# Recording the mixing's instructions and ordering them with a list scheduler; the output projection in two rounds

## The chip, the cores and the metric

The kernel runs on one core of one Trainium2 chip. The metric is the device time of one execution in microseconds (us). The engines are TensorE (PE, with its weight loads PEld), VectorE (DVE), ScalarE (ACT), GpSimd (POOL) and SyncE (SP), which here only starts transfers. Each engine works through a queue of its own in a fixed order, and waits at the head of it until the work that the instruction needs is done.

## The reference

One step of a trunk of two layers, for 128 context tokens and 256 latent tokens of width 1024 (T = 384 tokens in all). A layer is a gated feed-forward half step (FFN), a token mixing, and a second FFN half step. Abridged to what matters here, the mixing is:

```python
a_q, a_k, a_v, b_q, b_k, b_v, b_g, b_r, c_q, c_k, c_v = jnp.split(h @ lp['w_in'], offs, axis=-1)
a_q = rms_norm(a_q.reshape(B, T, A_HEADS, A_HEAD_DIM), lp['g_a_q'])     # also a_k, c_q, c_k
...
out_a = gqa_attention(a_q, keys_a, vals_a)                              # 6 heads of 64
o_b, s_f, s_b = gla_bidir(b_q, b_k, b_v, log_a[:, :, 0], log_a[:, :, 1], s0[:, 0], s0[:, 1])
out_b = rms_norm(o_b, lp['g_gla']) * jax.nn.silu(b_r)                   # 4 heads, keys 32, values 64
out_c = rms_norm(diff_attention(c_q, keys_c, vals_c, lam), lp['g_c_out']) * (1.0 - lam_init)
out = jnp.concatenate([out_a, out_b, out_c], axis=-1) @ lp['w_out']
```

Everything is float32. The output is y for both groups of tokens, the new caches and the states of the gated linear attention (GLA).

## The kernel before

The program is ffn, mixing, ffn for each layer, one after the other. The large products are done with split numbers: `load_split` (line 297) loads a weight tile `wraw`, ACT rounds it to a high part `whi` (line 303) and DVE subtracts to get the low part `wlo` (line 304); `mm3` (line 307) then adds three matmuls, high by high, high by low and low by high. Such a product has `whi` or `wlo` among its names and uses the whole array of 128 by 128.

The mixing (line 561) consists of named stages. "br bq bk bv" and "wa wv wq wk" are input projections; "ha hb" make the normalised tokens `h`; "lg de st" make the decays and states of the GLA, "L0" to "L6" its scores by seven levels of halving (`gla_level`, line 912) and "go" its output; "ra rq rk" are norm and rotary embedding; "p0a" to "p2b" and "o0" to "o2" are the attention of mixer A, "ax cx c0" to "c3", "n0 n1 s0 s1" that of mixer C. The stages are called in the order of the list `ORDER` (line 63, one list for each layer), and the output projection (from line 1070) follows: for each of eight tiles of 128 outputs, nine pieces of the mixed tokens are multiplied in one accumulation, in the order of `KORD`, with two weight loads (320 KB and 256 KB).

The attention and GLA use plain float32 matmuls, many of them on a part of the array only. A profile names the part before the shape. `32*64` stands for 32 rows and 64 columns: the GLA scores (line 902, six for each head and level) and part of its output (lines 960, 963). `64*128` are the attention scores (lines 732, 742, 776, 790). `128*64` are the products with the values of A and of the GLA (lines 757, 759, 957), and `128*32` are a few GLA products (lines 849, 882). Transposes (lines 721, 1003, 1036) and the products of mixer C with its values (lines 802, 804) use all rows and more than 64 columns, as the split products do. A plain float32 matmul leaves two records in the trace, a transpose or a split product one. The PSUM tiles that the matmuls write to are called `mm`, `ax`, `both` and `ada`; they are eight banks in all.

Other lines that the change touches: `newton` (line 312) computes 1/sqrt of small tiles on DVE with 13 instructions; `rsq_bcast` (line 331) and `qk_norm` (line 656) call it. `gla_level` takes four differences of prefix sums on DVE (lines 924 to 927). `a_probs` scales the probabilities on DVE (line 747, chosen by `NRM`). `add_x` (line 421) adds a finished output tile to the residual with two DVE instructions (line 423). `make_rstd` (line 374) is called ahead of the stages.

The instructions of the stages were given to the Tile framework in the order of the program, and each engine's queue came from that.

Of the kernel before, what the change touches and what calls it, by code (L numbers as in the profile page):

```python
# [17 lines left out]
P = 128  # L18
# [17 lines left out]
# column layout of the constant pack (shape constants)  # L36
# [6 lines left out]
# column layout of the small input pack  # L43
# [12 lines left out]
# modulation vectors computed beside each FFN: vectors, units left for the down part, steps of either part  # L56
# [4 lines left out]
NRM = (0, 1)  # L61
HV = (1, 1, 1, 1, 1, 1, 1, 1)
ORDER = (
    ("ha br bq hb bk wq bv lg rq de wk st L0 rk L1 cx wa wv L2 c0 L3 c1 L4 c2 ra L5 L6 n0 s0 c3 n1 p0a ax "
     "s1 p0b p1a go o0 p1b p2a o1 p2b o2").split(),
    ("br ha hb bq bk bv lg L0 wq rq wk de L1 st rk L2 wa cx wv L3 c0 ra L4 c1 c2 L5 c3 n0 L6 p0a p0b ax "
     "p1a o0 go s0 p1b p2a p2b o1 n1 s1 o2").split(),
)
KORD = (
    ("c0 c1 c2 c3 b0 b1 a0 a1 a2").split(),  # L70
    ("a0 b0 b1 c0 c1 a1 c2 c3 a2").split(),
)
# [9 lines left out]
def _build(ctx, tc, nc, I, O):  # L82
    V, S, G, PE = nc.vector, nc.scalar, nc.gpsimd, nc.tensor

    const = ctx.enter_context(tc.tile_pool(name="const", bufs=1))
    xp = ctx.enter_context(tc.tile_pool(name="xp", bufs=1))
    hp = ctx.enter_context(tc.tile_pool(name="hp", bufs=NHP))
    wp = ctx.enter_context(tc.tile_pool(name="wp", bufs=1))
    np_ = ctx.enter_context(tc.tile_pool(name="nrm", bufs=1))
    ps_mm = ctx.enter_context(tc.tile_pool(name="psm", bufs=3, space=PSUM))  # L90
    ps_ax = ctx.enter_context(tc.tile_pool(name="psx", bufs=3, space=PSUM))
    ps_ad = ctx.enter_context(tc.tile_pool(name="psa", bufs=1, space=PSUM))

    # eight banks: three for products, three for the rest, one for either (turn), one for the modulation
# [19 lines left out]
    nc.sync.dma_start(out=cc, in_=I["sp"][:, S_C:S_C + 16])  # L114
# [12 lines left out]
    def load_consts(i):  # L127
        for t, n, c in ((sp, "sp", S_GV), (cst, "cst", K_BON)):
            cols = slice(c, None) if i else slice(0, c)
            nc.sync.dma_start(out=t[:, cols], in_=I[n][:, cols])  # L130

    def load_consts2(w):
# [6 lines left out]
        # -(exp(lq1 . lk1) - exp(lq2 . lk2) + init)  # L139
# [12 lines left out]
    # ---------------------------------------------------------------- adaLN  # L152
# [39 lines left out]
    def cond_rows_pe(pool):  # L192
# [6 lines left out]
        for r in (0, 32):  # L199
            nc.sync.dma_start(out=cb[r:r + 1], in_=I["cb"][0:1])  # L200
# [1020 lines left out]
```

## Time and profile before

| | before |
|---|---|
| time, median of 3 runs (lowest, highest) | 1599.53 us (1589.74, 1602.13) |
| span of the profiled execution | 1590.9 us |
| PE busy over the span | 1556.5 us (98%) |
| DVE, ACT, POOL busy | 1236.2, 726.6, 196.5 us |
| the two mixings, from 317 to 536 us and from 1096 to 1311 us | 219 and 215 us |
| an FFN between them, 536 to 818 us | 282 us |

The page gives no time for the profiled execution other than its span. A matmul's record lasts until its result has been written, so the records of successive matmuls overlap; how long one of them keeps PE is the time from its start to the start of the next. PE "busy" therefore says little by itself: a stretch in which no new matmul starts for 0.3 us still counts as busy.

### The profile page before, as it was taken

How to read it: one execution, taken by the hardware profiler on the slowest of the kernel's cores; microseconds unless marked ns; L12 is line 12 of the kernel's file. 1: busy time of each engine (PE TensorE's matmuls, PEld its weight loads, DVE VectorE, ACT ScalarE, POOL GpSimd, SP SyncE). 2: the span in 40 equal slices, each digit the busy share in tenths (PEclk: the TensorE clock that was granted, in tenths of full speed). 3: DMA queues.
4: the chain of work that ended last, by engine and by line, in shares of the span. 5: the costliest groups of instructions: out<-in, count | busy, mean ns of one | idle time of the engine just before them, and what ended most of it. 6: DMA issues, size and time to landing. Idle time of an engine off the chain costs nothing.

```text
span 1590.9 us, 25045 instructions
## 1 busy us (share of the span) xinstructions
PE 1556.5 (98%) x9370; PEld 1457.3 (92%) x9370; DVE 1236.2 (78%) x2318; ACT 726.6 (46%) x1420; POOL 196.5 (12%) x239
## 2 busy tenths in 40 slices
PE   7999999999999999999999999999999999999999
PEld 4999999987667999999999999999875599999999
DVE  4799999888876788988968988676897867666532
ACT  4544433356566544443344444334646554444321
POOL 1111130031000211111001111101100011111100
PEclk9999999999899999999999999999999999999999
DMA  8666677533103465566655556543321064433441
GB/s 327 222 228 227 226 225 253 182 98 114 48 7 130 163 204 198 198 196 198 216 212 202 196 198 203 178 136 117 116 77 39 1 232 148 143 133 132 124 139 56
DMA packets 83229, 256.37 MB, mean 161 GB/s; under 512 B 10978, under 2 KB 19746, under 8 KB 82722
## 3 DMA queue, kind: packets, MB, share of 16 engines
q1 hardware_dynamic: 83108, 254.78, 48.2%
q8 instruction: 73, 1.20, 0.3%
q14 instruction: 48, 0.39, 0.1%
HBM read 251.99 MB, written 2.75 MB: 160 GB/s over the span
## 4 chain that ended last, share of the span: by engine, by line
PE 88%; DVE 7%; ACT 2%; issue 1%; DMA 1%; POOL 1%; SPq 0%; DVEq 0%; ACTq 0%; POOLq 0%
PE mm L308 20%; PE mm L309 20%; PE mm L310 20%; PE both L308 6%; PE both L310 6%; PE both L309 6%; DVE wlo L304 1%; PE mm L742 1%; PE mm L790 1%; DVE t L686 1%; PE ax L721 1%; DVE junk L254 1%; PE ax L804 1%; PE ax L902 0%; ACT p L697 0%
## 5 line engine op out<-in xcount | busy, mean ns | idle before, releaser
L303 ACT ACTIVATE whi<-wraw 128x1024 fp32r<-128x1024 f32 (+4 forms) x358 | 348.3, 974 | 457.3 <-PE mm L309 265.5
L304 DVE TENSOR_TENSOR wlo<-wraw,whi 128x1024 fp32r<-128x1024 f32 (+4 forms) x358 | 452.4, 1266 | 132.6 <-ACT whi L303 131.4
L310 PE MATMUL mm<-h,wlo 128*128 128x386 f32 x1112 | 379.2, 341 | 2.3 <-DVE wlo L304 2.3
L308 PE MATMUL mm<-h,whi 128*128 128x386 f32 x1112 | 378.4, 341 | 2.8 <-POOL h L367 1.4
L309 PE MATMUL mm<-h,whi 128*128 128x386 f32 x1112 | 377.9, 340 | 0.5 <-POOL h L367 0.3
L254 DVE SCALAR_TENSOR_TENSOR junk<-araw,cb 128x1024 f32<-128x1024 f32 x256 | 312.6, 1221 | 0.8
L308 PEld LDWEIGHTS mm<-h,whi 128*128 128x128 f32 x1112 | 210.8, 190 | 5.0 <-ACT whi L303 1.9
L310 PEld LDWEIGHTS mm<-h,wlo 128*128 128x128 f32 x1112 | 211.0, 190 | 3.9 <-DVE wlo L304 3.3
L309 PEld LDWEIGHTS mm<-h,whi 128*128 128x128 f32 x1112 | 211.1, 190 | 2.1 <-POOL h L367 0.8
L477 POOL TENSOR_TENSOR alo<-s,ahi 128x384 fp32r<-128x384 f32 x88 | 115.6, 1314 | 641.7 <-ACT ahi L475 615.1
L309 PE MATMUL mm<-alo,whi 128*128 128x384 f32 x528 | 177.9, 337 | 0.0
L310 PE MATMUL mm<-ahi,wlo 128*128 128x384 f32 x528 | 177.9, 337 | 0.0
L308 PE MATMUL mm<-ahi,whi 128*128 128x384 f32 x528 | 177.9, 337 | 0.0
L308 PE MATMUL both<-h,whi 128*128 128x386 f32 x344 | 117.0, 340 | 0.0
L310 PE MATMUL both<-h,wlo 128*128 128x386 f32 x344 | 116.7, 339 | 0.0
L309 PE MATMUL both<-h,whi 128*128 128x386 f32 x344 | 116.5, 339 | 0.0
L475 ACT ACTIVATE ahi<-s 128x384 fp32r<-128x384 f32 x88 | 46.3, 526 | 129.4 <-DVE s L472 129.3
L308 PEld LDWEIGHTS mm<-ahi,whi 128*128 128x128 f32 x528 | 99.2, 188 | 0.0
L309 PEld LDWEIGHTS mm<-alo,whi 128*128 128x128 f32 x528 | 99.2, 188 | 0.0
L310 PEld LDWEIGHTS mm<-ahi,wlo 128*128 128x128 f32 x528 | 99.2, 188 | 0.0
L308 PE MATMUL mm<-whi,h 128*128 128x384 f32 (+2 forms) x240 | 86.6, 364 | 6.2 <-ACT bc L418 4.4
L309 PE MATMUL mm<-wlo,h 128*128 128x384 f32 (+2 forms) x240 | 85.8, 358 | 0.3 <-DVE wlo L304 0.3
(366 smaller groups left out, 2331.5 us busy)
## 6 DMA issues: line engine op xcount, KB each, us to landing
wraw<-in_wgu SPq DMA_DIRECT2D x170, 512.0 KB, 4.2
araw<-in_w_adat SPq DMA_DIRECT2D x128, 512.0 KB, 3.9
wraw<-in_wd SPq DMA_DIRECT2D x64, 512.0 KB, 4.2
wraw<-in_wd SPq DMA_DIRECT2D x32, 384.0 KB, 3.6
araw<-in_w SPq DMA_DIRECT2D x16, 512.0 KB, 5.7
wraw<-in_wo SPq DMA_DIRECT2D x16, 320.0 KB, 2.8
wraw<-in_wit SPq DMA_DIRECT2D x8, 512.0 KB, 3.5
wraw<-in_wa SPq DMA_DIRECT2D x8, 512.0 KB, 3.6
```

The lines of the kernel that those rows point to most:

```text
L254: V.scalar_tensor_tensor(out=junk, in0=w, scalar=1.0, in1=self.cb[:, c, :], op0=ALU.mult, op1=ALU.mult, accum_out=self.acc[:, f, c:c + 1])
L303: S.activation(out=hi[:, :cols], in_=raw[:, :cols], func=AF.Copy)
L304: vi = V.tensor_tensor(out=lo[:, :cols], in0=raw[:, :cols], in1=hi[:, :cols].bitcast(F32), op=ALU.subtract)
L308: PE.matmul(ps, lhsT=lh, rhs=rh, start=start, stop=False)
L309: PE.matmul(ps, lhsT=lh, rhs=rl, start=False, stop=False)
L310: return PE.matmul(ps, lhsT=ll, rhs=rh, start=False, stop=stop)
L475: S.activation(out=hi, in_=s, func=AF.Copy)
L477: G.tensor_tensor(out=lo, in0=s, in1=hi.bitcast(F32), op=ALU.subtract)
L686: V.tensor_tensor(out=rv[:, :, :, a, :], in0=sv[:, :, :, 1 - a, :], in1=nv[:, None, :, a, :].to_broadcast([P, n, 2, m]), op=ALU.mult)
L721: pi = PE.transpose(ps[:, i * P:(i + 1) * P], p[:, i, :], ident)
L742: PE.matmul(ps, lhsT=qta[r, i, (t + 1) * P:(t + 2) * P], rhs=kta[r, :], start=True, stop=True)
L790: PE.matmul(pp[m], lhsT=qtc[r, h, (t + 1) * P:(t + 2) * P], rhs=ktc[r, h, 0:T], start=True, stop=True)
```

## The change

Inside `mixing`, every engine call is now recorded instead of issued. At the end of the mixing a list scheduler goes through the recorded instructions: it keeps the dependencies and the number of buffers, holds a duration for each kind of instruction (`cost`), and picks at each step, among the instructions that can start earliest on their engine, the one recorded first. The instructions are then issued in that order, and each is chained to the one before it on its engine. The FFNs are issued as before.

The stages of both layers have one new list. The eight tiles of the output projection are computed in two rounds: stages "q0" to "q7" multiply the four pieces of mixer C while the attention is still running, and add the result to the residual; the last part of the mixing multiplies the other five pieces and adds again. In `proj_m` the loop over the three token tiles now lies outside the loop over k. `rsq_act` takes the place of `newton` in `rsq_bcast` and `qk_norm`: exp and ln on ACT, and one step of Newton's rule. The four differences of a GLA level go from DVE to POOL, and the scaling of A's probabilities from DVE to ACT.

```diff
-NRM = (0, 1)
+NRM = (1, 1)
...
-    ("ha br bq hb bk wq bv lg rq de wk st L0 rk L1 cx wa wv L2 c0 L3 c1 L4 c2 ra L5 L6 n0 s0 c3 n1 p0a ax "
-     "s1 p0b p1a go o0 p1b p2a o1 p2b o2").split(),
...
+    ("bk ha br bq hb wq rq wk bv lg rk L0 L1 L2 de wa cx wv L3 ra L4 c0 c2 c1 c3 L5 n0 n1 p1a p0a st s0 s1 "
+     "p1b q7 L6 q3 ax p0b o0 q5 go q2 p2a p2b o1 q1 q6 q4 o2 q0").split(),
+) * DEPTH
...
+KR = 4
...
+        while ready:
+            best, start = None, {}
+            for op in ready:
+                s = slot(op)
+                if s is not None:
+                    start[op] = max(s, op.ready, free.get(op.eng, 0.0))
...
+            low = {}
+            for op, s in start.items():
+                low[op.eng] = min(low.get(op.eng, 1e18), s)
+            for op, s in start.items():
+                if s <= low[op.eng]:
+                    key = (low[op.eng], -rank(op), op.n)
+                    if best is None or key < best[0]:
+                        best = (key, op)
...
+def rank(op):
+    return -op.n
...
+    if op.eng == "PE":
+        if op.name == "transpose":
+            t = 0.109
+        elif op.kw["rhs"].dtype == F32R:
+            t = 0.452e-3 * no
+        else:
+            k = op.kw["rhs"].shape[0]
+            t = 1.68e-3 * no * (0.6 if k <= 64 else 1.0)
+            if k == 32:
+                t = 0.04
+        op.busy, op.late = t, t + 0.2
+        return
...
+    def rsq_act(pool, ss, n, scale, parts, tag):
...
+        V.tensor_scalar(out=mh, in0=ss, scalar1=-0.5 * scale, scalar2=-0.5 * EPS, op0=ALU.mult, op1=ALU.add)
+        y = pool.tile([P, n], F32, tag=tag + "y", bufs=2, name="ny")[:parts]
+        S.activation(out=y, in_=mh, func=AF.Ln, scale=-2.0)
+        S.activation(out=y, in_=y, func=AF.Exp, scale=-0.5)
...
+        V.tensor_tensor(out=a, in0=y, in1=y, op=ALU.mult)
+        V.tensor_tensor(out=a, in0=a, in1=mh, op=ALU.mult)
...
+        V.scalar_tensor_tensor(out=y2, in0=a, scalar=1.5, in1=y, op0=ALU.add, op1=ALU.mult)
...
-                    for k in range(k0, k0 + kper):
-                        c = (k - k0) * n
-                        for t in range(3):
+                    for t in range(3):
+                        for k in range(k0, k0 + kper):
+                            c = (k - k0) * n
...
-                V.tensor_tensor(out=ev[:, 0, :, :, 1, :], in0=cut(c0, 1)[:, :, :, 1, :], in1=mid(c0), op=ALU.subtract)
...
+                G.tensor_tensor(out=ev[:, 0, :, :, 1, :], in0=cut(c0, 1)[:, :, :, 1, :], in1=mid(c0), op=ALU.subtract)
...
+            def wo_round(m, k0, k1, parts):
+                mo = [{"a": moa, "b": mob, "c": moc}[n[0]][int(n[1])] for n in KORD[l][k0:k1]]
+                ps = mmps()[:, :T]
+                for a, b in parts:
+                    w = load_split(I["wo"][l, m][:, a * P:b * P], (b - a) * P)
...
+            for m in range(KT):
+                stages[f"q{m}"] = lambda m=m: add_x(l, 1, m, wo_round(m, 0, KR, ((0, KR),)))
...
+                end_tile(l, 1, m, wo_round(m, KR, 9, ((KR, 9),)), acc, nxt, None)
             us = [make_u(*nxt, k) for k in range(KT)]
+            rec.run()
```

The recorded instructions of the changed kernel all carry the line of the recorder that issues them (358), so they are told apart by their tiles.

PE, among the first layer's projections, where the scores of the GLA levels (`e`) stand beside a projection of 512 columns (`whi,h`). Before:

```order
L310 MATMUL mm<-whi,h 128x512
L308 MATMUL mm<-whi,h 128x512
L902 MATMUL ada<-e 64x64 x6
L902 MATMUL ax<-e 64x64 x18
L1036 MATMUL both<-cst,t_4125 128x128 x4
L309 MATMUL mm<-wlo,h 128x512
L310 MATMUL mm<-whi,h 128x512
```

Changed:

```order
L358 MATMUL both<-e 64x64
L358 MATMUL ada<-e 64x64
L358 MATMUL ax<-e 64x64 x2
L358 MATMUL mm<-whi,h 128x512
L358 MATMUL both<-e 64x64
L358 MATMUL ada<-e 64x64
L358 MATMUL ax<-e 64x64 x2
L358 MATMUL mm<-whi,h 128x512
L358 MATMUL ax<-e 64x64 x2
L358 MATMUL mm<-wlo,h 128x512
```

The 24 scores of a level stood in one block between the projection's products; now two to four of them stand between each product and the next.

PE, first layer, the products of the first pieces of the output projection (`chi`, `clo`, `ohi`, `olo`) beside the last attention products (`pt,av` with the values, `kta,qta` scores). Before:

```order
L757 MATMUL ada<-ptx,av 64x128 x2
L759 MATMUL ada<-pt,av 64x256 x6
L721 MATMUL ax<-cst,p 128x128 x3
L757 MATMUL ax<-ptx,av 64x128 x2
L759 MATMUL ax<-pt,av 64x256
L309 MATMUL mm<-olo,whi 128x384
L310 MATMUL mm<-ohi,wlo 128x384
```

Changed:

```order
L358 MATMUL ax<-pt,av 64x256
L358 MATMUL mm<-de,s_3272 64x128
L358 MATMUL mm<-clo,whi 128x384
L358 MATMUL ax<-pt,av 64x256
L358 MATMUL mm<-chi,wlo 128x384
L358 MATMUL mm<-kta,qta 128x384
L358 MATMUL mm<-chi,whi 128x384
L358 MATMUL mm<-kta,qta 128x384
L358 MATMUL ax<-e,cst 128x384
```

Products with the values that stood in rows of two and six are now separated by single products of the output projection's first round.

POOL, first layer, after the rotary multiplications of mixer C's keys (`t<-t,cst`). Before, and then changed:

```order
L1026 MEMSET t_4150 128x8x16
L681 TENSOR_TENSOR t_4153<-t_3993,cst 128x384
L681 TENSOR_TENSOR t_4811<-t_4351,cst 128x512
L681 TENSOR_TENSOR t_4826<-t_4357,cst 128x512
L942 COPY sc_3326<-sd_3324 64x6x64 x2
```

```order
L358 TENSOR_TENSOR t_4001<-t_3866,cst 128x384
L358 TENSOR_TENSOR e<-c_3274 128x3x64 x2
L358 TENSOR_TENSOR e<-c_3274 128x6x32
L358 TENSOR_TENSOR e<-c_3278 128x3x64 x2
L358 TENSOR_TENSOR e<-c_3278 128x6x32
```

The differences of the seven levels (28 instructions for each layer) now stand in POOL's queue, ahead of the rotary multiplications of mixer A.

## Rows read from the trace of the kernel before

**Rows 1.** Windows: length, PE, PEld, DVE, ACT, POOL busy (instructions), PEclk, DMA share, GB/s.

```profile
536.00:818.00 282.00, 282.00 (x1594) 281.56 (x1593) 243.33 (x389) 117.02 (x210) 33.80 (x39) 1.00 0.58 192
317.00:536.00 219.00, 210.94 (x1438) 167.81 (x1437) 171.40 (x440) 127.63 (x289) 28.69 (x40) 0.96 0.29 92
1096.00:1311.00 215.00, 205.61 (x1437) 163.88 (x1436) 172.05 (x440) 126.68 (x288) 26.65 (x40) 0.98 0.29 95
390.00:410.00 20.00, 20.00 (x137) 16.30 (x138) 17.12 (x38) 9.59 (x26) 0.00 (x0) 0.83 0.24 74
430.00:450.00 20.00, 19.93 (x142) 10.21 (x141) 13.86 (x40) 11.10 (x29) 0.00 (x0) 0.74 0.05 15
1210.00:1230.00 20.00, 19.67 (x116) 11.21 (x116) 12.39 (x37) 13.64 (x38) 0.00 (x0) 0.83 0.00 1
```

**Rows 2.** Chain that ended last, from 1228 to 1262 us: start, length, what.

```profile
1229.21 0.55 PE ax L721 x3
...
1239.53 0.84 PE mm L742 x2
...
1255.53 0.84 PE mm L742 x2
```

**Rows 3.** Timeline of PE, second layer's attention: start, length, instructions, array part, shape.

```profile
1235.44 0.32 PE L902 MATMUL both<-e 32*64 32x64 f32 x2
1235.70 0.55 PE L721 MATMUL ada<-cst,p 128*128 128x128 f32 x3
1236.18 0.56 PE L902 MATMUL both<-e 32*64 32x64 f32 x10
...
1238.97 0.56 PE L902 MATMUL ada<-e 32*64 32x64 f32 x12
1239.46 0.91 PE L742 MATMUL mm<-kta,qta 64*128 64x384 f32 x2
1240.30 0.89 PE L808 MATMUL ax<-pt,cst 96*96 96x384 f32 x2
```

**Rows 4.** Timeline of PE, whole-array products that follow each other.

```profile
1260.03 0.81 PE L972 MATMUL both<-e,cst 128*128 128x384 f32 x2
1260.67 0.49 PE L721 MATMUL ada<-cst,p 128*128 128x128 f32 x3
1261.00 0.82 PE L721 MATMUL ax<-cst,p 128*128 128x128 f32 x6
```

**Rows 5.** Timeline of PE, split products ahead of and behind partial ones.

```profile
1158.52 0.34 PE L309 MATMUL mm<-wlo,h 128*128 128x384 f32 x1
1158.70 0.34 PE L310 MATMUL mm<-whi,h 128*128 128x384 f32 x1
1158.97 0.74 PE L902 MATMUL ax<-e 32*64 32x64 f32 x30
...
377.87 0.50 PE L310 MATMUL mm<-whi,h 128*128 128x512 f32 x1
378.21 0.40 PE L308 MATMUL mm<-whi,h 128*128 128x512 f32 x1
378.44 0.39 PE L309 MATMUL mm<-wlo,h 128*128 128x512 f32 x1
```

**Rows 6.** Groups by line, 317 to 536 us: busy us, mean ns, idle before.

```profile
L924 DVE TENSOR_TENSOR e<-c 128x192 f32<-128x192 f32 x7 | 2.4, 344 | 0.0
L327 DVE SCALAR_TENSOR_TENSOR ny<-na,ny 128x24 f32<-128x24 f32 (+2 forms) x21 | 3.7, 177 | 0.4
L747 DVE TENSOR_SCALAR p<-p,rs 128x384 f32<-128x384 f32 x12 | 4.9, 412 | 0.1
L795 ACT ACTIVATE p<-p,rs 128x384 f32<-128x384 f32 x8 | 4.9, 610 | 0.0
L423 DVE SCALAR_TENSOR_TENSOR x<-mm,mod,x 128x128 f32<-128x128 f32 (+1 forms) x12 | 4.4, 412 | 2.6 <-PE mm L310 2.6
L681 POOL TENSOR_TENSOR t<-t,cst 128x384 f32<-128x384 f32 x4 | 5.8, 1439 | 11.5 <-DVE t L1032 11.5
```

More of the change, by code (lines that the diff above doesn't have):

```diff
@@ L69, with _strided, _regroup, parse @@
 KORD = (
     ("c0 c1 c2 c3 b0 b1 a0 a1 a2").split(),
-    ("a0 b0 b1 c0 c1 a1 c2 c3 a2").split(),
-)
+) * DEPTH
+KR = 4
+def _strided(v, shape, strides):
+    return np.lib.stride_tricks.as_strided(v, shape, strides)
+def _regroup(v, pat, kw):
+    lhs, rhs = [p.replace("(", " ( ").replace(")", " ) ").split() for p in pat.split("->")]
+    def parse(t):
+        out, g = [], None
+        for x in t:
+            if x == "(":
+                g = []
+            elif x == ")":
+                out.append(g)
+                g = None
+            elif g is not None:
+                g.append(x)
+            else:
+                out.append([x])
+        return out
+    dim = {}
+    for names, n, st in zip(parse(lhs), v.shape, v.strides):
+        known = math.prod(kw[x] for x in names if x in kw)
+        for x in reversed(names):
+            c = kw[x] if x in kw else n // known
+            dim[x] = (c, st)
+            st *= c
+    shape, strides = [], []
+    for names in parse(rhs):
+        c, st = 1, 0
+        for x in reversed(names):
+            n, s = dim[x]
+            if n == 1:
+                continue
+            assert c == 1 or s == st * c, (pat, "not one stride")
+            if c == 1:
+                st = s
+            c *= n
+        shape.append(c)
+        strides.append(st)
+    return _strided(v, shape, strides)
@@ new lines, with __init__, first, start @@
+class Cell:
+    def __init__(self, make, shape, tag):
+        self.make, self.tag = make, tag
+        self.view = np.empty(shape, np.int8)
+        self.ap, self.uses, self.left = None, [], 0
+    def first(self):
+        return self.uses[0][0].n
+class Tag:
+    def __init__(self, name, bufs):
+        self.name, self.bufs, self.fixed, self.cells = name, bufs, [], []
+    def start(self):
+        self.cells = sorted((c for c in self.cells if c.uses), key=Cell.first)
+        held = [f for f in self.fixed if f.left]
+        self.fixed, self.next = held, 0
+        self.free = [0.0] * (self.bufs - len(held))
+        for c in self.cells + held:
+            c.tag = self
@@ new lines, with cost @@
+STATS = []
+HOP = 0.04
+SPARE = {'ax': 1}
+def rank(op):
+    return -op.n
+def cost(op):
+    o = op.outs[0]
+    n = max(math.prod(x.shape[1:]) for x in [o] + [i for i in op.ins if len(i.shape) > 1])
+    no = math.prod(o.shape[1:])
+    lag = 0.0
+    if op.eng == "SP":
+        op.busy, op.late = 0.06, 2.2 + o.shape[0] * no * 4 / 250e3
+        return
[4 more added lines that the diff above has]
+            t = 0.452e-3 * no
+        else:
+            k = op.kw["rhs"].shape[0]
[3 more added lines that the diff above has]
+        op.busy, op.late = t, t + 0.2
+        return
+    if op.eng == "DVE":
+        if n <= 32:
+            t = 0.16
+        elif op.name == "tensor_scalar":
+            t = 0.27 + 0.0004 * n
+        elif op.name == "scalar_tensor_tensor":
+            t = max(0.2 + 0.00106 * n, 0.14 + 0.00105 * n)
+        else:
+            t = 0.15 + 0.00105 * n
+        op.busy, op.late = t - 0.05, t
+    elif op.eng == "ACT":
+        t = 0.16 if n <= 4 else 0.2 + 0.00083 * n
+        if op.kw.get("accum_out") is not None:
+            t += 0.2
+        op.busy, op.late = t - 0.06, t
+    else:
+        t = 0.15 if n <= 4 else 0.15 + 0.0032 * n if op.name == "tensor_tensor" else 0.15 + 0.001 * n
+        op.busy, op.late = t, t + 0.05
@@ L430, in end_tile @@
         if nxt is None:
-            nc.sync.dma_start(out=O["y"][m], in_=x[m])
+            SY.dma_start(out=O["y"][m], in_=x[m])
         else:
```

269 lines of the change are left out of this document (220 added, 49 removed).

## The prediction

> **What bounds the kernel now.** I first looked at the stretches of the program, by windows. The FFNs keep PE busy without a gap: 282.00 of 282 us in the one shown [rows 1], and nothing in them changes but their borders. So the change is decided in the two mixings, 219 and 215 us [rows 1]. There PE is busy 210.94 and 205.61 us, DVE 171.4 and 172.1, ACT about 127, POOL under 29. The reader is to see two kinds of loss of PE: idle time, 219 - 210.9 = 8.1 and 215 - 205.6 = 9.4 us, and time at the lower of its two clock levels. The granted clock was 0.83, 0.74 and 0.83 in the three stretches of 20 us that are shown; the means of the mixings, 0.96 and 0.98, leave nothing for the others. Against full clock these lose (0.17 + 0.26) x 20 = 8.6 us in the first mixing and 3.4 us in the second. What PE has to do at full clock is then 219 - 8.1 - 8.6 = 202 us, and 215 - 9.4 - 3.4 = 202 us. That is an upper value, since waits that are shorter than the overlap of two records don't show as idle; the lower value is some us less, and I take 202.
>
> Hence at most 17 + 13 = 30 us can be won by a better order if PE's work stays what it is. The chain of waits says the same: from 1229.21 to 1255.53 us, in the attention of the second layer, it runs through PE alone [rows 2]. This kernel's mixing is close to bound by PE, and the question is what the new order does to PE's own work.
>
> **What one matmul costs PE.** The time from one start to the next in the timeline [rows 3 to 5] gives two prices for the same instruction. Three transposes among other whole-array products take 1261.00 - 1260.67 = 0.33 us; between products on parts of the array they take 1236.18 - 1235.70 = 0.48. Six GLA scores in a block take 1239.46 - 1238.97 = 0.49 us, one alone 1235.70 - 1235.44 = 0.26, so that five more cost 0.23, or 0.05 each, and being there at all costs 0.21. One attention score (two records of 384 columns) takes 1240.30 - 1239.46 = 0.84, where two records of 384 columns with the whole array on both sides take 1260.67 - 1260.03 = 0.64. A split product ahead of a GLA score holds PE for 1158.97 - 1158.70 = 0.27 instead of 0.18, and the first split product behind one 378.21 - 377.87 = 0.34 instead of 378.44 - 378.21 = 0.23. So each **visit** to another part of the array (a row of instructions on one part, between instructions on others) costs, beyond its work: 0.09 + 0.11 = 0.20 us if it is whole-array work that begins with a split product, 0.15 if it begins with a transpose, about 0.20 for 32x64 and for 64x128. For 128x64 and 128x32 no row is shown; between the lowest and the highest of these I take the lowest, 0.15, which they share with the transposes in that they have all 128 rows.
>
> **The change part by part.** *Order of PE.* The instructions of PE are the same in kind and number; only the order differs. I counted the visits in the two orders, in the first mixing and (in brackets) the second. Before: 38 (37) to the whole array, of which 8 (9) begin with a split product; 20 (26) to 32x64, 19 (20) to 64x128, 12 (11) to 128x64, 4 (4) to 128x32. Changed: 144 (149), of which 84 (95) with a split product; 100 (98), 36 (40), 30 (31), 19 (16). The recorder's scheduler has no price for a visit, and it takes the earliest recorded among the instructions that are ready, so it deals split products and small ones out in turn. The increase costs 76 x 0.20 + 30 x 0.15 + 80 x 0.20 + 17 x 0.20 + 33 x 0.15 = 44 us in the first mixing, and 86 x 0.20 + 26 x 0.15 + 72 x 0.20 + 20 x 0.20 + 32 x 0.15 = 44 us in the second. PE's work becomes 202 + 44 = 246 us in each.
>
> The bounds of this term: if only the leaving of a part is paid, which the 0.27 against 0.18 us shows as 0.09, 236 more visits cost 21 us; at the highest price, 0.21 for all, 50 us. Two matmuls on different parts that run beside each other save something in blocks of the same kind (the products with A's values now stand alone), and save something in the new order too (scores of four heads side by side); I take both together as nothing, with 4 us to either side.
>
> A rule of the Trainium skill bears on it (TensorEngine Tiling (Array Packing), Key Properties): a change of the tiling mode, not of the tile alone, drains TensorE. By a drain alone only the leaving would be paid, 21 us instead of 44 for each mixing; the rows show a dearer first instruction as well [rows 3, 5], and the measurement decides.
>
> *Waits.* In 246 us the other engines have room: DVE loses 28 x 0.344 us (differences to POOL), 9 of 13 instructions at six places where 1/sqrt is taken, 54 x 0.177, and 12 x 0.412 (scaling of A), and gains 16 x 0.412 for the second adding to the residual: 171.4 - 9.6 - 9.6 - 4.9 + 6.6 = 154 us [rows 1, 6]. ACT gains 12 x 0.61 = 7.3 and 12 small ones, between nothing and as much again: 135 to 142. POOL gains 28 differences of 192 columns, each between half of 1.44 us and all of it (that row has 384 columns): 20 to 40 us, so 49 to 69 [rows 1, 6]. A level's four differences thus take 2.9 to 5.8 us where DVE took 1.4. ACT's exp of that level waits for them, and behind them in POOL's queue stand the rotary multiplications of A; what hides both is PE's work on the projections. If that cover were gone, it would cost 1.5 to 4.4 us for each of seven levels. I expect PE's idle time and its time at the lower clock to go almost wholly, because a slower PE gives every other engine more time; I leave 2 us, between 0 (the FFN's windows) and the 17 us of now.
>
> *Edits at no cost.* The loads of the output weights are the same 16 for each mixing with the same bytes, moved earlier on SP's queue; the DMA engines are at 0.05 and 0.00 where they now fall [rows 1]. Their roundings and subtractions on ACT and DVE are as many as before. The turned loop of the projections changes only which of three banks is next.
>
> *The sum.* A mixing takes 246 + 2 = 248 us: 29 more than 219 and 33 more than 215, **62 us in all**. The profiled execution has a span of 1590.9 us (no other time is given for it), near the lowest run, 1589.74, and 0.5% under the median, 1599.53. 1590.9 + 62 = 1653, 1599.5 + 62 = 1661; I forecast the middle, **1657 us**.
>
> **The rivals.** *The waits go and the visits are free (chance 0.13).* The order fills PE's idle time and the clock stays up, and the price of a visit is hidden because the next weights or the next operands are late anyway. For it: PE does wait, 17 and 13 us. Against it: the prices in rows 3 were read where PE alone was on the chain, so nothing else was late there. Time: 1599.5 - 30 = 1570 us. The point from which it decides is the price of a visit: below 17 / 236 = 0.07 us the change wins. It would be faster.
>
> *Only the leaving is paid (0.13).* This is the drain of the page named above as the whole price. A mixing takes 202 + 21 + 2 = 225 us, 6 and 10 more than before: 1615 us, at the border of what counts as slower. The dearer first instructions of rows 3 and 5 speak against it. I give 0.09 of it to no change.
>
> *A queue in the wrong order (0.12).* PE comes later than the scheduler's table assumes; an instruction that stands at the head of DVE's, ACT's or POOL's queue then waits for PE while one behind it could go, and PE later waits for that one. The place is the GLA levels, where POOL's differences, ACT's exp, DVE's product and PE's scores follow each other seven times. Price: waits as large as now, 13 to 17 us for each mixing instead of 2: about 1657 + 26 = 1685 us.
>
> That the order isn't carried out as recorded is no rival: the two orders above are those of the programs as built.
>
> **How the numbers follow.** The forecast has a chance of 0.62. About 1% is what a measurement of this kernel can tell from no change. Slower by more: 0.62 + 0.12 + 0.04 = 0.78; no change: 0.09; faster: 0.13. The forecast's own range goes from 0.15 us for every visit (35 us, 44 in all: 1640) to 0.21 with 4 us of lost overlap (54 us, 82 in all: 1680). The range for 8 in 10 takes in the second and third rival and leaves out the first: 1612 to 1690 us.
>
> **What would show it.** In the changed profile, the windows of the mixings should be 240 to 255 us long, with PE busy nearly all of it, the clock at 1.00, DVE near 154 and POOL near 50 us, and the FFNs as long as now. In the timeline, a lone GLA score between two split products should hold them 0.46 us further apart than they stand without it (0.26 + 0.09 + 0.11). I would be wrong if split products that stand behind partial ones start 0.18 us apart, or if the mixings last less than 219 us; then visits are cheaper in this order than in the rows I read.

## The result, and the profile after

The changed kernel takes 1822.66 us (median of 4 runs, 1817.47 to 1829.90), the kernel before 1600.83 us beside it (4 runs): a ratio of **1.139, 95% interval 1.133 to 1.146**. I had forecast 1657 us and a range up to 1690. The direction was right; the loss is 222 us where the sum had 62.

First the windows of the changed kernel (columns as in [rows 1]): the two mixings, each from the last product of the FFN before it to the first gate product of the next, and the FFN between.

```profile
312.30:641.40 329.10, 314.24 (x1441) 202.60 (x1440) 167.91 (x365) 137.58 (x316) 45.56 (x68) 0.77 0.22 69
1201.20:1535.60 334.40, 317.97 (x1441) 202.83 (x1441) 167.88 (x366) 138.91 (x316) 45.78 (x67) 0.76 0.21 68
641.40:922.00 280.60, 280.60 (x1588) 280.13 (x1588) 243.73 (x389) 116.92 (x209) 33.23 (x40) 1.00 0.60 193
```

The FFN is as long as before. The mixings are 329 and 334 us long where they were 219 and 215 [rows 1]: 229 us together, all of the loss. Each length falls into three parts: PE's idle time (length less busy), time lost to the lower clock (length times one less the granted clock, as if a microsecond at the lower level, 1.2 GHz, did half the work of one at 2.4), and the rest, PE's work at full clock. This is an estimate by halving; what the same instructions took at both levels is measured further below, and moves some of the loss from the clock to the work. Before [rows 1]: 8.1 + 8.8 + 202.2 and 9.4 + 4.3 + 201.3 us. After: 14.9 + 75.7 + 238.5 and 16.4 + 80.3 + 237.7. Of the 229 us, by this estimate, **143 are the lower clock**, 73 PE's work, 14 idle time.

By stage, the first mixing of the changed kernel:

```profile
312.30:330.00 17.70, 8.70 (x27) 6.46 (x26) 12.61 (x32) 5.14 (x8) 3.07 (x3) 0.61 0.65 222
330.00:460.00 130.00, 125.21 (x714) 95.34 (x712) 83.05 (x147) 60.13 (x132) 32.89 (x41) 0.92 0.25 76
461.00:503.00 42.00, 42.00 (x135) 19.85 (x130) 15.80 (x48) 16.01 (x44) 1.90 (x4) 0.51 0.02 7
503.00:527.00 24.00, 23.84 (x152) 12.55 (x151) 13.92 (x39) 14.80 (x43) 0.00 (x0) 0.99 0.01 1
527.00:605.00 78.00, 78.00 (x231) 37.78 (x229) 19.72 (x51) 20.67 (x54) 2.27 (x4) 0.50 0.06 18
605.00:641.40 36.40, 35.48 (x184) 30.08 (x184) 22.25 (x48) 19.82 (x35) 5.44 (x16) 1.00 0.57 197
```

From 461 to 503 and from 527 to 605 us the clock is 0.51 and 0.50 while PE is busy in every microsecond, and DVE and ACT work for 38% of the time in the first and a quarter in the second. (The second mixing has two such stretches as well, from 1356 to 1400 and from 1411 to 1492 us.) The chain of waits of the second stretch confirms that PE waits for nobody:

```profile
by line: PE mm L358 56.4%; PE ax L358 26.2%; PE ada L358 11.8%; PE both L358 6.1%; issue 0.0%
```

The timeline of PE in the two stretches, between them and at the end (columns as in [rows 3]) shows what it does there:

```profile
480.43 1.65 PE L358 MATMUL mm<-ktc,qtc 64*128 64x384 f32 x2
482.01 0.90 PE L358 MATMUL ax<-cst,p 128*128 128x128 f32 x3
...
523.78 0.44 PE L358 MATMUL mm<-chi,wlo 96*128 96x384 f32 x1
524.15 0.30 PE L358 MATMUL ax<-bv,e 128*32 128x64 f32 x2
...
552.39 0.69 PE L358 MATMUL mm<-de,s 32*64 32x128 f32 x2
553.00 0.69 PE L358 MATMUL mm<-chi,wlo 96*128 96x384 f32 x1
553.62 0.68 PE L358 MATMUL mm<-de,st 32*64 32x128 f32 x2
554.24 0.69 PE L358 MATMUL mm<-chi,whi 96*128 96x384 f32 x1
...
605.58 0.34 PE L358 MATMUL mm<-chi,wlo 96*128 96x384 f32 x1
605.76 0.52 PE L358 MATMUL mm<-clo,whi 96*128 96x384 f32 x2
606.12 0.34 PE L358 MATMUL mm<-chi,whi 96*128 96x384 f32 x1
```

The two stretches are not alike. From 461 to 503 us there is no split product: GLA scores and transposes in turn, then the attention of mixer C. From 527 to 605 us split products stand alone between small matmuls, and each takes 553.62 - 553.00 = 0.62 us. One that stood alone at 523.78 us, while the clock was still up, took 524.15 - 523.78 = 0.37. At 605 us products stand in rows, the clock is back, and two of them take 606.12 - 605.76 = 0.36 us. The first stretch ended without a split product, after scores, products with the values and transposes.

### The profile page after: what moved, and what is told of

Its sections match the earlier page's. It is cut to its first block, busy times and chain, and to the rows that moved or that the text cites. A ratio compares the mean times of both kernels' runs of the same rounds, so it can differ in the third digit from the quotient of the medians.

```text
span 1817.6 us, 25038 instructions
## 1 busy us (share of the span) xinstructions
PE 1769.5 (97%) x9370; PEld 1527.2 (84%) x9370; DVE 1224.2 (67%) x2162; ACT 743.9 (41%) x1468; POOL 231.7 (13%) x295
## 4 chain that ended last, share of the span: by engine, by line
PE 92%; DVE 3%; ACT 1%; DMA 1%; issue 1%; SPq 0%; POOL 0%; DVEq 0%; ACTq 0%; POOLq 0%
PE mm L205 44%; PE mm L358 20%; PE both L205 15%; PE ax L358 7%; PE both L358 3%; PE ada L358 2%; PE ax L205 1%; DVE junk L205 1%; DVE wlo L205 1%; DVE t L358 0%; PE ada L205 0%; DMA araw<-in_w 0%; DMA wraw<-in_wit 0%; DMA wraw<-in_wgu 0%; DVE h L358 0%
## 5 line engine op out<-in xcount | busy, mean ns | idle before, releaser
L205 PE MATMUL mm<-h,whi 128*128 128x386 f32 x2096 | 542.3, 340 | 2.6 <-POOL h L205 1.4
L205 DVE TENSOR_TENSOR wlo<-wraw,whi 128x1024 fp32r<-128x1024 f32 (+2 forms) x278 | 376.0, 1354 | 100.0 <-ACT whi L205 97.5
L205 ACT ACTIVATE whi<-wraw 128x1024 fp32r<-128x1024 f32 (+2 forms) x278 | 282.5, 1017 | 377.3 <-PE mm L205 236.0
L205 PEld LDWEIGHTS mm<-h,whi 128*128 128x128 f32 x2096 | 384.5, 189 | 6.1 <-issue 1.7
L205 PE MATMUL both<-h,whi 128*128 128x386 f32 x688 | 177.7, 339 | 0.0
L358 PE MATMUL mm<-whi,h 128*128 128x384 f32 (+2 forms) x480 | 145.7, 394 | 3.3 <-ACT bc L358 2.0
L205 PEld LDWEIGHTS both<-h,whi 128*128 128x128 f32 x688 | 125.9, 189 | 1.2 <-issue 1.2
L358 ACT ACTIVATE whi<-wraw 128x1024 fp32r<-128x1024 f32 (+4 forms) x80 | 66.0, 827 | 133.8 <-PE mm L358 112.3
L358 PEld LDWEIGHTS mm<-whi,h 128*128 128x128 f32 x480 | 89.1, 200 | 19.5 <-ACT bc L358 3.1
L358 DVE TENSOR_TENSOR wlo<-wraw,whi 128x1024 fp32r<-128x1024 f32 (+4 forms) x80 | 76.8, 964 | 38.3 <-ACT whi L358 38.3
```

Source lines behind the costliest of these rows:

```text
L205: return rec.add(key, name, f, a, k) if rec.on else f(*a, **k)
L358: ins = op.fn(*map(un, op.args), **{q: un(v) for q, v in op.kw.items()}).ins
```

## The experiments

T1 stands for: the visits to parts of the array cost time and make the granted clock fall by themselves. T2: other parts of the change (POOL's differences, 1/sqrt and scaling on ACT, the two rounds) make PE wait, and the waiting lowers the clock.

**Small matmuls in an FFN that waits for nothing** (on the kernel before; `dm` is a free bank):

```diff
+    def extra(kind, n=1):
+        for _ in range(n):
+            if kind < 4:
+                PE.matmul(dm[0][0:64, 0:64], lhsT=cst[0:32, 0:64], rhs=cst[0:32, 0:64], start=True, stop=True)
+            else:
+                PE.matmul(dm[0][:, 0:16], lhsT=cst[:, 0:128], rhs=cst[:, 0:16], start=True, stop=True)
...
+                lone = {(0, 1): (1, 3)[m > 10], (1, 1): (4, 6)[m > 10]}.get((l, i), 0)
...
+                if (l, i) == (1, 0):
+                    extra(0, (16, 48)[m > 10])
```

> The kernel before with small matmuls added to the gate and up products of three FFNs (their results are not used); no work on another engine is added, so nothing new is waited for. FFN of layer 0 after the mixing: one lone 32x64 score-like matmul behind every third split product in tiles 0 to 10 (176), behind every product in tiles 11 to 21 (528). FFN of layer 1 ahead of the mixing: the same numbers, but in blocks of 16 and 48 at a tile's end. FFN after it: lone whole-array matmuls of 16 columns, again 176 and 528. Eleven plain tiles take about 92 us. T1 (visits cost time and by themselves make the granted clock fall): first stretch +28 to +46 us, second +85 to +137 us at full clock, and at least the second at 0.5, so 300 us or more; in blocks +14 and +42 us, whole-array +10 and +30 us, both at clock 1.00. Total 1900 to 2150. T2 (the clock fell because PE waited for other engines): the first two stretches cost the price of the visits at most, clock 1.00 throughout; total below 1880.

2412.02 us. Windows of 7 tiles with a lone score behind every third product, 8 with one behind every product, 6 with 16 scores in a block, 8 with 48 in a block, 9 and 7 with lone whole-array matmuls:

```profile
592.70:702.50 109.80, 109.80 (x561) 74.05 (x560) 52.95 (x77) 24.90 (x50) 9.51 (x7) 1.00 0.31 106
813.50:1205.00 391.50, 391.50 (x1153) 219.37 (x1152) 59.25 (x86) 30.27 (x56) 11.03 (x9) 0.50 0.10 34
1382.00:1446.00 64.00, 64.00 (x482) 62.10 (x480) 45.64 (x67) 21.51 (x42) 8.21 (x6) 1.00 0.46 158
1483.00:1626.00 143.00, 143.00 (x1158) 139.94 (x1156) 61.35 (x87) 28.49 (x56) 10.81 (x8) 0.79 0.29 96
1995.00:2104.00 109.00, 109.00 (x725) 109.00 (x724) 50.04 (x71) 32.30 (x64) 10.47 (x9) 1.00 0.31 107
2123.00:2257.00 134.00, 134.00 (x1008) 134.00 (x1007) 38.56 (x54) 25.79 (x49) 8.11 (x7) 1.00 0.16 56
```

A tile takes 15.7, 48.9, 10.7, 17.9, 12.1 and 19.1 us; a plain one 8.5 (shown below). A lone score at full clock costs (15.7 - 8.5) / 16 = 0.45 us, as the prediction had it (0.46); in a block of 16 it costs 0.14. A lone whole-array matmul of 16 columns, which is no visit, costs (12.1 - 8.5) / 16 = 0.23, so at most about half of the 0.45 hangs on the part of the array (the score has more columns too). With a score behind every product the clock is 0.50 although nothing was added to any other engine. So T2's cause is not needed. But T1 missed two points: the blocks of 48, with one visit for each tile, drop to 0.79, where it had 1.00, and the stretches cost more than it said (11 tiles of the first 79 us in place of 28 to 46), so that the total lies above its 2150.

**A price for a visit in the changed kernel's scheduler** (0.2 us; with it, one tag may be taken out of turn and a matmul with few rows is costed in full, which was not tried by itself):

```diff
                     start[op] = max(s, op.ready, free.get(op.eng, 0.0))
+                    if op.eng == "PE" and part(op) != last_part:
+                        start[op] += VISIT
...
+            if op.eng == "PE":
+                last_part = part(op)
...
+VISIT = 0.2
...
+def part(op):
+    a = op.args[1] if op.name == "transpose" else op.kw["lhsT"]
+    rows, cols = a.shape[0], a.shape[1]
+    return None if rows > 64 and cols > 64 else (rows, cols)
...
-SPARE = {'ax': 1}
+SPARE = {'ax': 1, 'e': 1}
...
-            t = 1.68e-3 * no * (0.6 if k <= 64 else 1.0)
+            t = 1.68e-3 * no
```

> The changed kernel, its scheduler made to see what a visit costs: 0.2 us are added to the start of an instruction on PE that uses another part of the array than the last one, and a split product with few rows is costed in full; the pools are the same, one tag more may be taken out of turn. Visits per mixing 104 and 87 in place of 329 and 334 (before: 93 and 98); everything else of the change stays. T1: the mixings come down from 333 and 336 us to 215 to 240 and the granted clock is 0.5 in at most 25 us of each; total 1590 to 1650. T2: differences on POOL, norms on ACT and the two rounds hold PE up as they do now; total stays above 1750, with clock 0.5 for 100 us or more of a mixing.

1674.77 us, ratio 1.046 [1.041, 1.052]: two thirds of the loss are gone, with every other part of the change still in. The two mixings:

```profile
313.90:573.60 259.70, 227.69 (x1441) 175.98 (x1440) 168.59 (x368) 139.56 (x319) 44.59 (x68) 0.90 0.27 87
1134.60:1390.80 256.20, 222.44 (x1442) 173.24 (x1441) 168.65 (x366) 139.32 (x317) 46.35 (x68) 0.89 0.27 89
```

Idle 32.0 and 33.8, lower clock 26.0 and 28.2, work 201.7 and 194.3 us. The work is what it was before the change. T1 was right on that and too hopeful on the rest (it had 1590 to 1650): the clock and the waits of this order are still worse than before.

**The operations without the order** (on the kernel before):

```diff
-NRM = (0, 1)
+NRM = (1, 1)
...
-                y = newton(mp, ss.rearrange("p a b -> p (a b)"), 24, 1.0 / d, P, "q")
+                y = rsq_act(mp, ss.rearrange("p a b -> p (a b)"), 24, 1.0 / d, P, "q")
...
-                V.tensor_tensor(out=ev[:, 0, :, :, 1, :], in0=cut(c0, 1)[:, :, :, 1, :], in1=mid(c0), op=ALU.subtract)
...
+                G.tensor_tensor(out=ev[:, 0, :, :, 1, :], in0=cut(c0, 1)[:, :, :, 1, :], in1=mid(c0), op=ALU.subtract)
```

> The kernel before, with its own order and one round, and only the changed operations: reciprocal roots by ACT's logarithm and exponential, GLA differences on POOL, norm factors on ACT, a projection's loops turned. Visits as before. T1: 1590 to 1625, clock 0.98 to 1.00. T2: most of the 222 us are here, over 1700.

1608.79 us, ratio 1.006 [1.003, 1.009]; 11 us idle, clock 0.95 and 0.96, work 200.0 and 203.6 us a mixing. T2 falls: these parts together cost 8 us.

**One round of the output projection** in the changed kernel:

```diff
-     "p1b q7 L6 q3 ax p0b o0 q5 go q2 p2a p2b o1 q1 q6 q4 o2 q0").split(),
+     "p1b L6 ax p0b o0 go p2a p2b o1 o2").split(),
...
-                end_tile(l, 1, m, wo_round(m, KR, 9, ((KR, 9),)), acc, nxt, None)
+                end_tile(l, 1, m, wo_round(m, 0, 9, ((0, 5), (5, 9))), acc, nxt, None)
```

> The changed kernel with the output projection in one round at the end, so that the scheduler has no split products of it to mix in. Visits 302 and 304 per mixing (329 and 334 with two rounds), those that end at a split product 54 and 60 (84 and 95). T1: 27 to 30 visits less at 0.14 us are 4 us a mixing, and somewhat less time at clock 0.5; total 1760 to 1815. T2 (the two rounds do it): total 1600 to 1680.

1809.56 us in one run: 18.6 and 20.5 us idle, 75.5 and 71.3 lost to the clock, work 234.3 and 232.3. The two rounds aren't the main cause.

**Does the change of part lower the clock, or how little PE streams?** The block of 48 asked for it. Again lone matmuls on the kernel before:

```diff
+            if kind == "half":
+                PE.matmul(d[0:64, 0:64], lhsT=cst[0:32, 0:64], rhs=cst[0:32, 0:64], start=True, stop=True)
+            elif kind == "whole":
+                PE.matmul(d[:, 0:16], lhsT=cst[:, 0:128], rhs=cst[:, 0:16], start=True, stop=True)
+            elif kind == "rows":
+                PE.matmul(d[:, 0:T], lhsT=cst[0:64, 0:128], rhs=cst[0:64, 0:T], start=True, stop=True)
+            else:
+                PE.matmul(d[0:64, 0:T], lhsT=cst[:, 0:64], rhs=cst[:, 0:T], start=True, stop=True)
...
+            if lone == "half":
+                extra(lone, cnt[0] % 2)
+            elif lone:
+                extra(lone, 4 if lone == "whole" else 1)
```

> The kernel before with other small matmuls added to the gate and up products of two FFNs (results unused), to tell what lowers the granted clock. T1a: changing the part of the array does. T1b: it is that PE, though busy by the records, streams little for its time, whether parts change or not. A plain tile takes 8.5 us. (A) FFN of layer 0, tiles 0 to 10: four whole-array matmuls of 16 columns behind every split product, no change of part: T1a clock 1.00; T1b 0.5. (B) the same FFN, tiles 11 to 21: a lone 32x64 score behind every second split product (24 a tile): at full clock 8.5 + 24 x 0.45 = 19 us a tile; both theories leave open whether the clock falls, between one in three (1.00) and one in one (0.50). (C) FFN of layer 1 after the mixing, tiles 0 to 10: a 64x128 matmul of 384 columns behind every product; (D) tiles 11 to 21: a 128x64 one of 384 columns: parts change as often as with the lone scores, but with six times the columns. T1a: 0.5 in both; T1b: 1.00 in both, 48 x (0.17 + 0.8) = 45 to 55 us a tile.

3904.03 us. The windows of A (9 tiles), B (9), C (10) and D (10):

```profile
737.00:1612.50 875.50, 875.50 (x3889) 875.50 (x3890) 69.21 (x101) 34.03 (x63) 12.25 (x9) 0.50 0.05 18
1645.00:1935.90 290.90, 290.90 (x866) 169.92 (x865) 68.74 (x99) 34.06 (x64) 12.42 (x10) 0.50 0.15 52
2610.80:3193.00 582.20, 582.20 (x1443) 230.95 (x1442) 53.40 (x78) 38.26 (x72) 11.40 (x10) 1.00 0.07 23
3193.00:3751.10 558.10, 558.10 (x1441) 181.00 (x1440) 52.87 (x79) 37.73 (x71) 11.41 (x10) 1.00 0.06 19
```

A never leaves the whole array and falls to 0.50; C and D change part at every instruction and stay at 1.00. So T1a falls and T1b fits: PE's records read "busy" throughout, and what differs is how much is streamed in that time. B settles nothing by itself: it came right behind A, with the clock already at 0.50, and a later experiment shows that this matters. A tile of C took 58.2 us, somewhat more than the 45 to 55 expected.

**Fewer or more visits** (VISIT = 0.1; VISIT = 0.5, with one tag of another name out of turn).

> As the version with a price of 0.2 us, with 0.1 us: visits 162 and 168 per mixing, half of the changed kernel's. T1: PE's work at full clock is 203 + 68 x 0.18 = 215 us a mixing, its waits 20 to 30 us, clock 0.5 for longer than with 104 and 87 visits: total 1680 to 1740. If visits had no part in it: as the changed kernel, over 1780.

> The same with a price of 0.5 us: visits 44 and 45 per mixing, half of those before the change. T1: PE's work at full clock 195 us a mixing or less, but its waits rise as instructions are held back for one another (40 to 60 us): total 1660 to 1720. If time followed the visits alone it would come below the kernel before: under 1590.

1710.45 us, 1.073 [1.064, 1.082], and 1699.67 us, 1.066 [1.057, 1.075]. All orders side by side, first and second mixing:

| kernel | visits | length | idle | lower clock | PE's work |
|---|---|---|---|---|---|
| before | 93, 98 | 219, 215 | 8.1, 9.4 | 8.8, 4.3 | 202.2, 201.3 |
| price 0.5 | 44, 45 | 267.8, 272.7 | 40.6, 47.5 | 37.5, 38.2 | 189.7, 187.0 |
| price 0.2 | 104, 87 | 259.7, 256.2 | 32.0, 33.8 | 26.0, 28.2 | 201.7, 194.3 |
| price 0.1 | 162, 168 | 281.9, 267.6 | 32.4, 29.4 | 42.3, 26.8 | 207.2, 211.5 |
| one round | 302, 304 | 328.4, 324.1 | 18.6, 20.5 | 75.5, 71.3 | 234.3, 232.3 |
| changed | 329, 334 | 329.1, 334.4 | 14.9, 16.4 | 75.7, 80.3 | 238.5, 237.7 |

PE's work (by halving, as above) follows the visits: from 45 to 332 it rises by 49.7 us, 0.17 us a visit. The time does not follow them alone: with the fewest visits PE waits most, and the clock is lower again.

**Would longer runs of products bring the clock back in the changed kernel?** First each short run made three long, then some ten runs a mixing made sixteen:

```diff
+            if split and nxt is not None and part(nxt) is not None and run < 3:
+                again[op] = 3 - run
...
+            if split and nxt is not None and part(nxt) is not None and gap > 30:
+                again[op] = 16 - run
```

> The changed kernel with its order kept, and work added on PE: where only one or two split products stand between instructions on another part of the array, the last of them is issued again, to make three (126 and 135 products more in the two mixings; they are added into the same sums, so the outputs are other than the reference's). Visits stay 329 and 334. At full clock the added products cost 261 x 0.174 = 45 us. T1b: the clock stays at 1.00 for most of the stretches where it is 0.5 now, which gives back more than the products cost: 1690 to 1780, faster than the changed kernel although it does more. T1a (the changes of part lower the clock, and they are as many): 1850 to 1920.

1887.84 us, 1.184 [1.175, 1.193]. T1b's range missed, and the time lies in that of T1a, though T1a had fallen with A, C and D: the 261 products cost 22.8 and 28.1 us of work in the two mixings and the clock loss stayed (92.1 and 79.6 us; 75.7 and 80.3 in the changed kernel). In the first mixing the clock was down from 473 to 643 us, and runs of three did not bring it back, though one score behind three products had kept it at 1.00 in the FFN. Hence a new theory, made after this miss, T-hold: what keeps the clock up need not bring it back.

> The kernel before with small matmuls between the gate and up products of two FFNs (results unused), by tiles, to see whether a pattern that keeps the clock at 1.00 also brings it back. FFN of layer 0 after the mixing, from tile 0: 2 plain; 2 with a lone 32x64 score behind every product (clock 0.50); 3 with one behind every third; 2 as the first; 3 with a 64x128 matmul of 384 columns behind every product; 2 as the first; 3 plain; 2 as the first; 3 with a score behind every sixth. FFN of layer 1 after the mixing: 2 plain; 7 with score, 128x64 of 384 columns, score, 64x128 of 384 columns behind every third product; 2 with a score behind every product; 11 as the 7. T-hold (once down, the clock needs more than what kept it up; that is why three products in a row did not bring it back in the changed kernel): the tiles with a score behind every third, which took 15.7 us at 1.00, stay at 0.50 for most of their length (25 us or more a tile), and the last 11 take 1.3 times as long as the 7 or more; plain tiles return to 8.5 us within the first. T-now (only what PE does at that time counts): third 15.7 us, 384 columns 58 us, the last 11 as the 7.

```diff
+                plan = {(0, 1): (2 * [0] + 2 * ["one"] + 3 * ["third"] + 2 * ["one"] + 3 * ["rows"] + 2 * ["one"] + 3 * [0] +
+                                 2 * ["one"] + 3 * ["sixth"]),
+                        (1, 1): 2 * [0] + 7 * ["mix"] + 2 * ["one"] + 11 * ["mix"]}
```

3430.42 us. Windows: 3 tiles "third" and 3 "rows", each behind "one"; the first and second plain tile and the first and second "sixth" behind "one"; 6 tiles "mix" from full clock, and 10 behind "one".

```profile
661.40:741.40 80.00, 80.00 (x242) 53.09 (x241) 21.65 (x31) 10.51 (x21) 4.06 (x3) 0.50 0.17 59
839.30:1155.10 315.80, 315.80 (x433) 112.92 (x432) 22.49 (x32) 11.51 (x22) 4.07 (x3) 0.50 0.05 15
1253.00:1263.00 10.00, 10.00 (x50) 9.96 (x49) 7.07 (x11) 2.62 (x6) 1.56 (x2) 0.85 0.39 127
1263.00:1271.50 8.50, 8.50 (x50) 8.50 (x49) 7.04 (x10) 3.69 (x7) 1.36 (x1) 1.00 0.43 159
1375.60:1390.60 15.00, 15.00 (x65) 11.98 (x64) 7.05 (x11) 2.92 (x7) 1.36 (x1) 0.77 0.31 97
1390.60:1402.70 12.10, 12.10 (x66) 9.54 (x64) 7.21 (x11) 3.54 (x8) 1.37 (x1) 1.00 0.42 130
2061.00:2335.80 274.80, 274.80 (x1058) 127.70 (x1057) 31.67 (x48) 21.35 (x42) 6.67 (x6) 1.00 0.08 27
2432.20:3250.00 817.80, 817.80 (x1761) 347.84 (x1760) 56.44 (x82) 36.73 (x72) 11.51 (x11) 0.50 0.04 13
```

T-hold holds at every point. The same tile with a score behind every third product takes 26.7 us here and 15.7 in the first experiment; "rows" 105.3 and 58.2; the mixture 45.8 from full clock and 81.8 when it was down before, for ten tiles on end. Plain products bring the clock back within one tile, those with a score behind every sixth within one as well.

These pairs also show what the lower level costs: the same tile takes 26.7 / 15.7 = 1.70, 105.3 / 58.2 = 1.81 and 81.8 / 45.8 = 1.79 times as long at 0.50, not twice. By the lowest and highest of these, an estimate, the clock's part of the 229 us is 118 to 128 us in place of 143, and PE's work 88 to 98 in place of 73: 0.19 to 0.21 us a visit.

> The changed kernel with its order kept, and work added on PE in ten places of each mixing: where a run of split products ends after more than 30 instructions of PE without a long run, its last product is issued again until 16 stand in a row (308 products more in all, added into the same sums, so the outputs are other than the reference's). Visits stay 329 and 334. At full clock the added products cost 308 x 0.19 = 58 us. T-hold: each block brings the clock back to 1.00 and it stays there for some microseconds, which repays a part of the blocks or all of them: 1740 to 1860, clock 0.5 for less than 110 us of a mixing (154 and 161 in the changed kernel). T-now: the blocks alone are faster, all else stays: 1870 to 1940.

1806.6 us, 1.126 [1.117, 1.136]: 308 products more than the changed kernel (1.139 [1.133, 1.146]) and no slower. Its mixings:

```profile
311.40:632.80 321.40, 306.73 (x1599) 213.45 (x1598) 168.08 (x365) 137.61 (x316) 45.51 (x68) 0.90 0.22 71
1192.60:1523.30 330.70, 313.25 (x1592) 218.34 (x1591) 168.83 (x366) 138.38 (x316) 44.29 (x67) 0.88 0.21 69
```

By halving, the lower clock costs 32.1 and 39.7 us in place of 75.7 and 80.3; the added work, 36.1 and 35.9 us, is paid in full by that. Two windows of the first mixing show where:

```profile
490.00:500.00 10.00, 10.00 (x21) 4.48 (x20) 4.46 (x12) 3.85 (x9) 0.00 (x0) 0.50 0.00 0
550.00:560.00 10.00, 10.00 (x65) 6.99 (x64) 5.95 (x16) 4.03 (x16) 1.01 (x2) 1.00 0.15 44
```

The long stretch with split products runs at 1.00; the one before it, which has no split product and so got no block, is at 0.50 as it was. So long rows bring the clock back in the changed kernel too, where rows of three did not. Whether they do it through the hold or by raising what PE streams on the whole, this run can't tell; the hold is shown in the FFNs.

**The start of the mixings.** In the changed kernel PE stands still there, as it did not before. Its SP queue and PE:

```profile
312.68 0.33 SPq L358 DMA_DIRECT2D s<-in_state  x1
...
315.88 1.79 SPq L358 DMA_DIRECT2D wraw<-in_wit  x4
```

```profile
314.99 1.65 PE L358 MATMUL ax<-acc,cst 128*128 128x384 f32 x2 [2.38 <-DVE acc L205]
323.01 1.01 PE L358 MATMUL mm<-h,whi 128*128 128x386 f32 x2 [6.37 <-ACT whi L358]
```

Six small loads, whose tiles wait for the FFN's memory, stand ahead of the first weights. The edit puts them behind, alone and with the price of 0.2:

```diff
 def rank(op):
-    return -op.n
+    late = op.eng == "SP" and isinstance(op.outs[0], View) and op.outs[0].cell.tag.name != "wraw"
+    return -op.n - (1000 if late else 0)
```

> The changed kernel with one rank altered: on SP's queue the six small loads of a mixing (state, cached keys and values, the decay weights), which wait until the FFN before has let go of its memory, stand behind the first five loads of projection weights, as they do in the kernel before, and not ahead of them. In the changed kernel PE is idle for 2.4 and 6.4 us at the start of the first mixing and its clock is 0.61 over the first 17.7 us; in the kernel before it is busy all of the 17.6 us at 1.00. T-queue (this place on SP's queue makes that loss): 9.0 us idle and 0.39 x 17.7 = 6.9 us at the lower clock go, and 8.8 and 5.1 us in the second mixing: 30 us less, 1785 to 1800. T-norm (PE waits for the norm's sums or the splits instead): 1815 to 1825.

> The version with a price of 0.2 us for a visit, with the same altered rank. T-queue: 1675 less 20 to 30 us: 1645 to 1655, still slower than the kernel before, since the small loads account for at most 16 of the 32 and 34 us that PE is idle in its mixings. T-norm: 1670 to 1680.

1829.92 us, 1.142 [1.132, 1.153], and 1668.85 us, 1.041 [1.034, 1.048]: no gain alone, and with the price 6 us, which the intervals do not tell from nothing. Both of T-queue's ranges missed. It named the place, but taking it away was not enough. The weights now arrive in time, and the next in line holds PE: the second product waits 3.90 us for DVE's subtraction `wlo`, which stands in DVE's queue behind the chain of 1/sqrt. The window of the start, PE, and DVE from the head of that chain:

```profile
312.70:330.40 17.70, 10.57 (x33) 8.13 (x32) 12.37 (x32) 3.25 (x6) 4.16 (x3) 0.61 0.30 92
```

```profile
321.98 0.69 PE L358 MATMUL mm<-h,wlo 128*128 128x386 f32 x1 [3.90 <-DVE wlo L358]
```

```profile
317.77 0.17 DVE L358 TENSOR_SCALAR nm<-ht 128x12 f32<-128x12 f32 x1
...
320.24 0.58 DVE L358 STREAM_TRANSPOSE rstd<-ny 128x384 f32<-128x384 f32 x1
320.74 1.18 DVE L358 TENSOR_TENSOR wlo<-wraw,whi 128x1024 fp32r<-128x1024 f32 x1
```

PE's idle time there went from 9.0 to 7.1 us and the clock is 0.61 as it was. The altered rank alone also moved other instructions (13 visits more in the first mixing), and there the lower clock, by halving, costs 93.7 us where it was 75.7; so that run does not price the start by itself. None of the versions beats the kernel before; the nearest is its own order with the new operations, 0.6% slower.

## Why the prediction was wrong

*PE's work:* right. 44 us more for each mixing were forecast; by halving it was 36, by the ratios measured in the FFNs 44 to 49. The price of a visit is 0.15 us in the changed kernel by halving (36.3 / 236), 0.17 over all orders, 0.19 to 0.21 by the ratios, inside the 0.15 to 0.21 read from [rows 3, 5]. The Trainium skill (TensorEngine Tiling (Array Packing), Key Properties) says that a change of the tiling mode drains TensorE. It gives no price; the prediction's reading of it, that only the leaving is paid, had 21 us for a mixing, which is too little.

*The step that failed:* "I expect PE's idle time and its time at the lower clock to go almost wholly, because a slower PE gives every other engine more time; I leave 2 us". The lower clock, forecast at nothing, costs 75.7 and 80.3 us by halving, 62 to 72 by the ratios. I had taken it for a consequence of waiting, and [rows 1] should have made me doubt that: from 430 to 450 us the clock was 0.74 and PE busy for 19.93 of 20 us, and from 390 to 410 it was busy all the time at 0.83. What preceded those falls should have been read. In the kernel before, there were waits ahead of them, of 1.3 and 1.7 us:

```profile
420.00:430.00 10.00, 8.68 (x64) 5.30 (x63) 9.88 (x26) 5.91 (x17) 1.78 (x2) 1.00 0.19 59
380.00:392.00 12.00, 10.34 (x135) 7.93 (x135) 11.10 (x26) 8.10 (x15) 3.42 (x3) 1.00 0.22 61
```

So there waiting may have had a part. In the first mixing of the changed kernel it had next to none in the long falls: the clock fell at 462 and at 527 us, and PE was busy for 10.00 us from 450 to 460 and for 23.84 of the 24 us ahead of the second. What stands ahead of and in them is small matmuls in turn, in the second with lone split products: PE busy, little streamed, clock down. The FFN runs show that such a stream lowers the clock without any wait, and that it then stays down under work that would have kept it up; the second fall lasted 78 us, until products stood in rows at 605 us. What ended the first, with no split product in it, stays open. A visit is dearer at the lower clock too: a lone score costs (48.9 - 26.7) / 32 = 0.69 us there and 0.45 at full clock.

The Trainium skill's page TensorE: Matmul & The Clock Gate (Part 1 and HAM oscillation) has the clock go by how busy PE has been and shows it falling in waits for transfers. This case's trace shows it down in a stretch without any wait as well (0.50 over 391.5 us, PE busy 391.50).

*Waits:* 2 us forecast, 14.9 and 16.4 measured, of which 9.0 of the first stand at the start of the mixing. That the loads are the same was said of the output weights; of the six small loads moved ahead of the projection weights nothing was said, nor of the norm's chain behind them. The rival of a queue in the wrong order had the size of the waits (13 to 17 us), by luck: it had the wrong place (the GLA levels) and other queues (those of DVE, ACT and POOL).

*The rest:* FFNs as long as before, ACT 138 and 139 us (135 to 142), POOL 46 (near 50). DVE takes 168 us, not 154: the operations alone saved it 11 us less than I reckoned (158.7 us in that version, which has no second adding to the residual).

*The rivals:* free visits and leaving alone are both refuted by PE's work, 238 us or more where they had 202 and 223. The range up to 1690 had no case in which the clock falls further.

## What to carry to other kernels

A list scheduler that fills an engine needs a price for what follows what: dealing products and small matmuls out in turn cost 0.15 to 0.21 us a visit, and more than that again through the clock. Where PE is busy in the records, still read its granted clock, stage by stage, and what it did before each fall: a fall with a full PE offers no wait that could be taken away. Small matmuls in blocks of 16 between rows of 48 products kept the clock at 1.00, and a row of 16 products brought it back; an order that does this with the kernel's own products, and without the waits of the orders with a price, was not built.

## What the runs showed of the hardware

- The granted clock falls to 0.50 with PE busy without a gap, and without a change of part (four whole-array matmuls of 16 columns behind each product); partial matmuls of 384 columns in their place keep 1.00.
- It has a memory: one and the same pattern of matmuls runs at 1.00 for 274.8 us or at 0.50 for 817.8 us, by what ran ahead of it. At 0.50 a tile takes 1.70 to 1.81 times as long as at 1.00.
- Adding 308 products to the changed kernel did not make it slower.
- What exactly PE's stream must have (columns, share of the array, gaps too short for the records) stays open, as does what brings the clock back without split products (at 503 us in the changed kernel), and what the waits of 32 us in the orders with a price are made of.
